# An expert unit on quarters of the array, half-height products for a state-space response, and another order of the last expert block

## The chip, the cores and the metric

The program runs on one core of a Trainium2 chip. The core has a matrix engine (TensorE, PE in the profile, its weight loads apart as PEld), VectorE (DVE), ScalarE (ACT), GpSimd (POOL), and SyncE (SP), which here issues nearly all DMA transfers. The metric is the device time of one execution in microseconds, and its median over runs.

## The reference

Two layers of a diffusion backbone, on 256 latent and 256 context tokens of width 1024, all in float32. Each layer has a mixer of four head groups (two-dimensional neighbourhood attention, grouped attention with rotary positions, a bidirectional diagonal state space, windowed attention with sinks) and a channel mixer. Layer 0 has a dense SwiGLU; layer 1, on the latent tokens alone, has eight experts, of which the router picks two for each token:

```python
logits = jnp.einsum('bld,de->ble', h, w_router, ...) + b_router.astype(F32)
top_val, top_idx = lax.top_k(logits, TOP_K)          # TOP_K = 2
top_w = jax.nn.softmax(top_val, -1)
for e in range(N_EXPERTS):                           # 8 experts, 1024 x 3584
    out = out + gate[..., e:e + 1] * _swiglu(h, w_gate[e], w_up[e], w_down[e])
```

with `_swiglu(h) = (silu(h @ w_gate) * (h @ w_up)) @ w_down`, and behind it a residual sum with a gate vector from the conditioning and a layer norm. The state space needs, for each of 16 channel groups, its response at offsets of up to seven steps in both directions, which the kernel makes from products of the powers of its poles with its input and output matrices.

## The kernel before

**Experts.** The experts are ranked by how many tokens they got. The tokens are gathered into 768 slots, six units of 128. A unit of one expert is whole: units 0, 2 and 3 (largest, second and third expert). Units 1, 4 and 5 are mixed, 64 slots of one expert and 64 of another; unit 1 holds what the largest has beyond 128 (capacity 192) and the smallest (64). What goes past the capacities would be computed by an overflow branch (`overflow`, a test on a register at L1673).

The 3584 hidden columns are cut into seven blocks of 512. In each block the units go in pairs, (1,0), (5,2), (4,3), each a call of `swiglu_units`: gate for both units, up for both, then silu, product, four transposes (L1630), and down. Block 0 goes (5), (4), (1,0), (2,3), the last block (1,0), (5,2), (3), (4). A weight tile is 128 x 2048 (1 MiB); an expert has six in a block. `load` (L1660) issues them on SP in the order of use, into a ring of nine buffers (`ring` in the profile), each freed by its last reader.

A mixed unit works in float32 straight from the ring (L1608): for each of eight k, two matmuls, one per expert, on 64 columns of the array each, 512 wide; each is two instructions in the trace. A whole unit needs its weights split in a high and a low part first, high on ACT (L1571), low on DVE (L1572), and takes three matmuls per k (L1595, L1596, L1598) on all 128 columns. Down has four k in two halves of the 1024 output columns, which DVE adds into `yacc` with the slot's gate (L1744). In block 5, POOL multiplies `yacc` by the layer's gate vector (L1750); in block 6, DVE multiplies each product by it first (L1747). `combine` (L1713) puts a finished unit's `yacc` back on the tokens by matmuls with `DT` (who sits in which slot) and DVE adds the sum to the residual; for the last unit PE loads the tokens into PSUM (L1767) and adds to them there (L1771), and the last layer norm follows.

The order on an engine is laid out by a scheduler when the program is built; `behind(*chain)` keeps the matmuls of successive steps in order.

**State space.** `s5_prep` makes the responses `Ks` for four groups of channels at a time: `CT` is made by six products, copied into an array `X` of fifteen offsets, the upper 64 partitions for one direction and the lower 64 for the other, and eight matmuls (L709) on four quarters of 32 columns give 240 columns, copied by DVE (L715).

**Ahead of layer 0**, the input is scaled and shifted in two halves of four row blocks each: ACT writes the result as the high part `xa` (L1828), DVE scales `xT` itself (L1829), and the low part `xb` is the difference (L1830). L283, L284 and L285 are the first projection's matmuls with these parts.

## Time and profile before

| | |
|---|---|
| median of 3 runs | 1944.35 us (1936.6 to 1945.28) |
| the profiled execution | 1943.62 us, its span 1941.8 us |
| PE busy | 1810.1 us, 93% of the span |
| DVE, ACT, POOL busy | 1071.2, 693.1, 420.8 us |
| DMA traffic | 508.57 MB, mean 262 GB/s |
| granted TensorE clock, mean | 0.967 of full speed |
| matmuls of the mixed units (L1608), gate and up, down | 302.2 and 161.8 us |
| waits of SP for a ring buffer in the expert layer | 448.1 us for L1608, 220.0 us for L1572 |

The expert layer runs from about 1001 to 1929 us. A window tells how busy each engine was in a stretch and what the DMA engines moved; a wait is put down to the engine that released it last; the chain is the succession of work, waits included, that ended last. Times in the rows below count from the span's start.

### The profile page before, as it was taken

Reading aid. Unit: us, or ns where it says so; the run is one execution under the profiler, and the core shown is the slowest. Engines: PE = TensorE matmul, PEld = TensorE weight load, DVE = VectorE, ACT = ScalarE, POOL = GpSimd, SP = SyncE. Lnnn points to the kernel's source line nnn. Section 1 sums busy time; section 2 is a strip of 40 time slices with the busy share of each in tenths; the row PEclk is TensorE's granted clock in tenths of the full one; section 3 lists DMA queues with packets and bytes.
Section 4 is the critical chain, followed back from the end, with each engine's and each line's share of the span. In section 5 each row is a group of like instructions: output and inputs, shape, how many; then the busy total and the mean of one; then the engine's idle time right before and its main releaser. Section 6 shows DMA issues by size and latency. Waiting matters only on the chain.

```text
span 1941.8 us, 23723 instructions
## 1 busy us (share of the span) xinstructions
PE 1810.1 (93%) x8634; PEld 1150.1 (59%) x8634; DVE 1071.2 (55%) x1715; ACT 693.1 (36%) x1077; POOL 420.8 (22%) x368
## 2 busy tenths in 40 slices
PE   6799989799999999899969999999999899999997
PEld 2576547778777777586654475554554454544553
DVE  7978544825456244849673383453543444554473
ACT  2245553422212222436623363342333333423340
POOL 3852232634342422522340000000000000021000
PEclk9899989899999999998979999999999999999999
DMA  8455831224534545251349987999999999999893
GB/s 315 151 164 195 290 133 65 102 95 144 187 133 165 177 172 190 76 188 52 122 164 371 417 333 324 423 420 407 422 400 422 369 379 421 409 398 421 349 378 133
DMA packets 111498, 508.57 MB, mean 262 GB/s; under 512 B 21776, under 2 KB 31632, under 8 KB 68368
## 3 DMA queue, kind: packets, MB, share of 16 engines
q1 hardware_dynamic: 111376, 507.01, 67.1%
q8 instruction: 69, 1.13, 0.2%
q14 instruction: 53, 0.43, 0.1%
HBM read 491.29 MB, written 15.66 MB: 261 GB/s over the span
## 4 chain that ended last, share of the span: by engine, by line
PE 79%; DVE 12%; DMA 3%; issue 2%; POOL 2%; ACT 1%; SPq 1%; DVEq 0%; POOLq 0%; ACTq 0%
PE ps L1608 24%; PE ps L283 8%; PE ps L284 8%; PE ps L285 8%; PE ps L1595 6%; PE ps L1598 6%; PE ps L1596 6%; PE ps L358 2%; PE ps L1096 1%; PE ps L1058 1%; PE ps L1057 1%; PE ps L1630 1%; DMA ring<-in_ada_w_dram 1%; PE ps L1114 1%; PE ps L1713 1%
## 5 line engine op out<-in xcount | busy, mean ns | idle before, releaser
L1572 DVE TENSOR_TENSOR whl<-ring,whl 128x1024 fp32r<-128x1024 f32 x252 | 307.3, 1254 | 114.3 <-ACT whl L1571 105.2
L1571 ACT ACTIVATE whl<-ring 128x1024 fp32r<-128x1024 f32 x252 | 258.0, 1054 | 234.9 <-PE ps L1596 128.8
L1608 PE MATMUL ps<-ring,xg 128*64 128x512 f32 x1344 | 302.2, 599 | 6.0 <-DMA ring<-in_moe_w_dram 6.0
L303 ACT ACTIVATE ring<-ring 128x1024 fp32r<-128x1024 f32 x114 | 120.0, 1059 | 312.7 <-PE ps L284 155.9
L283 PE MATMUL ps<-xa,ring 128*128 128x512 f32 (+1 forms) x576 | 217.2, 378 | 9.0 <-DVE xa L423 8.1
L285 PE MATMUL ps<-xa,ring 128*128 128x512 f32 (+1 forms) x576 | 216.7, 377 | 0.0
L284 PE MATMUL ps<-xb,ring 128*128 128x512 f32 (+1 forms) x576 | 216.2, 376 | 0.3 <-DVE xb L424 0.3
L1608 PEld LDWEIGHTS ps<-ring,xg 128*64 128x64 f32 x1344 | 94.6, 137 | 189.4 <-issue 186.4
L1750 POOL TENSOR_TENSOR yacc<-yacc,gate 128x1024 f32<-128x1024 f32 x6 | 21.1, 3512 | 766.9 <-DVE yacc L1744 734.9
L1608 PE MATMUL ps<-ring,mhT 128*64 128x512 f32 x672 | 161.8, 596 | 1.4 <-ACT mhT L1635 1.4
L305 DVE TENSOR_TENSOR ring<-ring,ring 128x1024 fp32r<-128x1024 f32 x76 | 106.0, 1397 | 90.9 <-ACT ring L303 90.5
L305 POOL TENSOR_TENSOR ring<-ring,ring 128x1024 fp32r<-128x1024 f32 x38 | 95.7, 2518 | 240.5 <-ACT ring L303 212.5
L1595 PE MATMUL ps<-whl,xhl 128*128 128x512 f32 x336 | 135.2, 402 | 0.0
L283 PEld LDWEIGHTS ps<-xa,ring 128*128 128x128 f32 x576 | 110.5, 192 | 36.1 <-DVE xa L423 8.5
L1596 PE MATMUL ps<-whl,xhl 128*128 128x512 f32 x336 | 131.2, 391 | 0.0
L1627 DVE TENSOR_TENSOR mh<-mh,ps 128x512 f32<-128x512 f32 x42 | 28.9, 687 | 185.3 <-PE ps L1608 159.9
L285 PEld LDWEIGHTS ps<-xa,ring 128*128 128x128 f32 x576 | 110.5, 192 | 24.4 <-issue 6.6
L284 PEld LDWEIGHTS ps<-xb,ring 128*128 128x128 f32 x576 | 110.3, 192 | 20.7 <-issue 2.8
L1598 PE MATMUL ps<-whl,xhl 128*128 128x512 f32 x336 | 104.2, 391 | 0.0
L1608 PEld LDWEIGHTS ps<-ring,mhT 128*64 128x64 f32 x672 | 48.4, 137 | 92.9 <-issue 90.6
L1744 DVE SCALAR_TENSOR_TENSOR yacc<-ps,mtab,yacc 128x512 f32<-128x512 f32 x60 | 45.0, 750 | 90.7 <-PE ps L1608 65.8
L1626 ACT ACTIVATE mh<-ps 128x512 f32<-128x512 f32 x42 | 25.0, 595 | 181.2 <-PE ps L1608 122.5
(445 smaller groups left out, 3026.6 us busy)
## 6 DMA issues: line engine op xcount, KB each, us to landing
ring<-in_moe_w_dram SPq DMA_DIRECT2D x334, 1024.0 KB, 10.5
ring<-in_ada_w_dram SPq DMA_DIRECT2D x96, 512.0 KB, 5.7
ring<-in_ffn_gu_dram SPq DMA_DIRECT2D x44, 512.0 KB, 3.5
ring<-in_w_in_dram SPq DMA_DIRECT2D x32, 512.0 KB, 4.7
ring<-in_ffn_d_dram SPq DMA_DIRECT2D x22, 512.0 KB, 3.8
ring<-in_w_out_dram SPq DMA_DIRECT2D x16, 512.0 KB, 3.9
s5CT<-CT SPq DMA_DIRECT2D x8, 512.0 KB, 3.4
s5WB<-WB SPq DMA_DIRECT2D x8, 512.0 KB, 3.0
```

The lines of the kernel that those rows point to most:

```text
L283: PE.matmul(o, a[0], b[0], start=start, stop=False)
L284: PE.matmul(o, a[0], b[1], start=False, stop=False)
L285: PE.matmul(o, a[1], b[0], start=False, stop=stop)
L303: S.activation(hi, r, AF.Copy)
L305: (G if cnt[0] % 3 == 0 else V).tensor_sub(lo, r, hi.bitcast(F32))
L1571: S.activation(t[:, 0], src, AF.Copy)
L1572: V.tensor_sub(t[:, 1], src, t[:, 0].bitcast(F32))
L1595: PE.matmul(o[:, :n], xh[:, k], wh[:, k - k0], start=k == 0, stop=False)
L1596: PE.matmul(o[:, :n], xl[:, k], wh[:, k - k0], start=False, stop=False)
L1598: m = PE.matmul(o[:, :n], xh[:, k], wl[:, k - k0], start=False, stop=k == nks - 1)
L1608: PE.matmul(o[a:b, :n], x[:, k, a:b], w_(w)[:, k - a0], start=k == 0, stop=k == nks - 1, tile_position=pos_)
L1744: V.scalar_tensor_tensor(d, y[hf], g, d, op0=ALU.mult, op1=ALU.add)
```

## The change

Three parts.

**Unit 1 on quarters.** The largest expert's capacity falls to 160 and the smallest's to 32. Unit 1 holds the 32 slots of each twice, in four quarters of 32. A quarter takes half of the 512 columns of a weight tile: quarters 0 and 1 the largest expert's, 2 and 3 the smallest's. `step` issues four matmuls for each k, on 32 columns of the array each, 256 wide; gate and up leave 256 columns for each slot of each quarter, two transposes follow, and `yacc` of unit 1 is 512 wide. `DT` gets a second plane for it, split by the parity of the quarter, and `combine` takes two matmuls of 256 where other units have one of 512.

**State space response.** No `X` and no mask: the products are taken for each direction on its own 64 partitions, 16 matmuls of half height into two PSUM tiles, 128 wide; ACT copies them together and DVE adds the shared offset. In the scaling ahead of layer 0, ACT scales in place and then copies the high part, 512 wide.

**Order.** The last block goes (1,0), (2,3), (5), (4). Combining the units of a finished call is issued between gate and up of the next one (`mid`), the load of the tokens into PSUM ahead of the last unit's transposes (`end`). The gate vector is spread in block 6, behind its first pair (and within the overflow branch), not in block 0; POOL's products in block 5 go, and in block 6 DVE multiplies the whole sum. The overflow branch claims five ring buffers instead of four.

```diff
...
-CAPS = (192, 128, 128, 64, 64, 64, 64, 64)
-BASE = (0, 256, 384, 512, 576, 640, 704, 192)
-NSLOT = sum(CAPS)
-NU = NSLOT // P
-
-UNITS = ((0, 0), (0, 7), (1, 1), (2, 2), (3, 4), (5, 6))
-
-WHOLE = {u for u, rk in enumerate(UNITS) if rk[0] == rk[1]}
+CAPS = (160, 128, 128, 64, 64, 64, 64, 32)
+BASE = (0, 256, 384, 512, 576, 640, 704, 160)
+
+
+UNITS = ((0, 0), (0, 0, 7, 7), (1, 1), (2, 2), (3, 4), (5, 6))
+NU = len(UNITS)
+QUART = {u for u, rk in enumerate(UNITS) if len(rk) == 4}
+
+WHOLE = {u for u, rk in enumerate(UNITS) if len(set(rk)) == 1}
+
+SLOTS = np.arange(NU * P)
+SLOTS[P : 2 * P] = P + np.repeat([0, 0, 32, 32], 32) + np.tile(np.arange(32), 4)
...
-            for i in range(2):
-                V.tensor_copy(X[0:64, i, :, 7:15, :], CT[0:64, i])
-                V.tensor_copy(X[64:128, i, :, 0:8, :], CT[64:128, i])
-            kp = ps("s5")
-            for i in range(2):
-                for g4 in range(4):
-                    PE.matmul(
-                        kp[32 * g4 : 32 * g4 + 32, :240], bb[:, i, 4 * q + g4, :],
-                        X[:, i, g4].rearrange("p m h -> p (m h)"), start=i == 0, stop=i == 1,
-                        tile_position=(0, 32 * g4),
-                    )
+            kp = [ps("s5"), ps("tr")]
+            for r in range(2):
+                dp = slice(64 * r, 64 * r + 64)
+                for i in range(2):
+                    for g4 in range(4):
+                        PE.matmul(
+                            kp[r][32 * g4 : 32 * g4 + 32, :P], bb[dp, i, 4 * q + g4, :],
+                            CT[dp, i, g4].rearrange("p k h -> p (k h)"), start=i == 0, stop=i == 1,
+                            tile_position=(64 * r, 32 * g4),
+                        )
             Ks = T([240], "Ks", nb)
-            V.tensor_copy(Ks, kp[:, :240])
...
+            S.activation(Ks[:, 112:240], kp[0][:, 0:128], AF.Copy)
+            S.activation(Ks[:, 0:112], kp[1][:, 0:112], AF.Copy)
+            V.tensor_add(Ks[:, 112:128], Ks[:, 112:128], kp[1][:, 112:128])
...
+        DT = mp.tile([P, NU + 1, 256], F32R, name="DT")
...
+                if u in QUART:
+                    for i, v in enumerate((u, NU)):
+                        V.tensor_scalar(DT[:, v], tp[:, 0:256], C("par")[:, i : i + 1], None, op0=ALU.mult)
+                else:
...
+                yacc[u] = mp.tile([P, 512 if u in QUART else D], F32, name=nm("yacc"))
...
+                if len(ws) == 2 and ws[0] is ws[1]:
+                    parts = [(0, 128, ws[0], None, slice(0, n))]
+                else:
+                    z = 128 // len(ws)
+                    parts = [
+                        (z * a, z * a + z, w_, (0, z * a), slice(n * (a % 2), n * (a % 2) + n) if z == 32 else slice(0, n))
+                        for a, w_ in enumerate(ws)
+                    ]
...
                 for k in ks:
                     with behind(*chain):
                         ms = [
                             PE.matmul(
-                                o[a:b, :n], x[:, k, a:b], w_(w)[:, k - a0], start=k == 0, stop=k == nks - 1, tile_position=pos_
+                                o[a:b, :n], x(k, a) if callable(x) else x[:, k, a:b], w_(w)[:, k - a0, c],
+                                start=k == 0, stop=k == nks - 1, tile_position=pos_,
                             )
-                            for a, b, w_, pos_ in halves
+                            for a, b, w_, pos_, c in parts
                         ]
...
+                if i == 0 and mid:
+                    mid()
+            if end:
+                end()
+            ys = [
+                [ps("mm" if u else "s5") for _ in range(4 // len(ws))] for u, (_, ws) in enumerate(units)
+            ]
...
+                if len(ws) == 4:
+
+                    hT = lambda k, a, hT=hT: hT[:, k % 2, a // 64 * 64 + k // 2 * 32 :][:, :32]
                 for hf in range(2):
-                    ms = step(ys[u][hf], hT, 4 + hf, ws, 0, range(nk), nk, 512)
+                    if len(ws) == 4:
+                        ms = step(ys[u][0][:, 256 * hf : 256 * hf + 256], hT, 4 + hf, ws, 0, range(nk), nk, 256)
+                    else:
+                        ms = step(ys[u][hf], hT, 4 + hf, ws, 0, range(nk), nk, 512)
...
+                gate = slots[4][:, :D]
+                bcast_rows(gate, adaT[1][:, 40:48, 0])
...
+            units = sorted(units, key=lambda u: u in QUART)
             for h in range(2):
                 for t in range(2):
                     o = ps("mm")
-                    for u in units:
-                        PE.matmul(
-                            o, DT[:, u, 128 * t : 128 * t + 128].bitcast(F32), yacc[u][:, 512 * h : 512 * h + 512],
-                            start=u == units[0], stop=u == units[-1],
-                        )
+                    with behind(*chain):
+                        for u in units:
+                            for c, v, d in ((0, u, 256), (256, NU, 512)) if u in QUART else ((0, u, 512),):
+                                chain[:] = [
+                                    PE.matmul(
+                                        o[:, c:d], DT[:, v, 128 * t : 128 * t + 128].bitcast(F32),
+                                        yacc[u][:, (d - c) * h : (d - c) * (h + 1)],
+                                        start=u == units[0], stop=u == units[-1] and d == 512,
+                                    )
+                                ]
...
+        acc = {}
+
+        def tokens():
+
+            for h in range(2):
+                for t in range(2):
+                    acc[t, h] = ps("tr" if t + h == 2 else "mm")
+                    with behind(*chain):
+                        chain[:] = [
+                            PE.matmul(acc[t, h], ident, res[t + 2][:, 512 * h : 512 * h + 512], start=True, stop=False)
+                        ]
...
-        order = {0: ((5,), (4,), (1, 0), (2, 3)), NB - 1: (PAIRS[0], PAIRS[1], (3,), (4,))}
+        order = {0: ((5,), (4,), (1, 0), (2, 3)), NB - 1: (PAIRS[0], (2, 3), (5,), (4,))}
...
-            ys = swiglu_units([(xg[u], [ws[r] for r in UNITS[u]]) for u in us], 4)
-            if todo:
-                combine(todo)
-                todo = []
+            ys = swiglu_units(
+                [(xg[u], [ws[r] for r in UNITS[u]]) for u in us], 4,
+                partial(combine, todo) if todo else None, tokens if tail else None,
+            )
+            todo = []
+            if (b, us) == (NB - 1, PAIRS[0]):
+                gate = mp.tile([P, D], F32, name="gate")
+                bcast_rows(gate, adaT[1][:, 40:48, 0])
+
+                gateq = mp.tile([P, 512], F32, name="gateq")
+                for a in range(4):
+                    r = slice(32 * a, 32 * a + 32)
+                    G.tensor_copy(
+                        gateq[r].rearrange("p (h x) -> p h x", h=2),
+                        gate[r].rearrange("p (h q x) -> p h q x", h=2, q=2)[:, :, a % 2],
+                    )
             for u, y in zip(us, ys):
                 g = gsl[:, u : u + 1]
-                for hf in range(2):
+                for hf in range(len(y)):
                     c = slice(512 * hf, 512 * hf + 512)
-                    d = yacc[u][:, c]
+                    d, gt = yacc[u][:, c], gateq if u in QUART else gate
                     if b == 0:
                         V.tensor_scalar(d, y[hf], g, None, op0=ALU.mult)
-                    elif b < NB - 1:
+                    else:
                         V.scalar_tensor_tensor(d, y[hf], g, d, op0=ALU.mult, op1=ALU.add)
-                    else:
-                        yg = wtile("mh")
-                        V.tensor_mul(yg, y[hf], gate[:, c])
-                        V.scalar_tensor_tensor(d, yg, g, d, op0=ALU.mult, op1=ALU.add)
-                if b == NB - 2:
-                    G.tensor_mul(yacc[u], yacc[u], gate)
+                    if b == NB - 1:
+                        V.tensor_mul(d, d, gt[:, c])
             if b == NB - 1:
                 todo = list(us)
-            if at == 2:
-                gate = mp.tile([P, D], F32, name="gate")
-                bcast_rows(gate, adaT[1][:, 40:48, 0])
             if (b, us) == (OVER, PAIRS[-1]):
-                overflow([mw() for _ in range(4)])
+                overflow([mw() for _ in range(5)])
...
-                    S.activation(hi[:, f, 256 - 256 * r : 512 - 256 * r], x, AF.Identity, bias=bi, scale=sc)
-                    V.tensor_scalar(x, x, sc, bi, op0=ALU.mult, op1=ALU.add)
+                    S.activation(x, x, AF.Identity, bias=bi, scale=sc)
+                S.activation(hi[:, f], xT[:, f], AF.Copy)
...
```

PE, gate of unit 1 in a middle block, the last of its eight k, and the first rows of unit 0. `ps` is the PSUM tile, `ring` the weight tile's buffer, `xg` the gathered tokens; each row is a matmul of two instructions. Before:

```order
L1608 MATMUL ps_9301<-ring_7757,xg 64x512
L1608 MATMUL ps_9301<-ring_7749,xg 64x512
L1608 MATMUL ps_9301<-ring_7757,xg 64x512
L1608 MATMUL ps_9301<-ring_7749,xg 64x512
L1608 MATMUL ps_9301<-ring_7757,xg 64x512
L1608 MATMUL ps_9301<-ring_7749,xg 64x512
L1595 MATMUL ps_9302<-whl_7758,xhl 128x512
L1596 MATMUL ps_9302<-whl_7758,xhl 128x512
L1595 MATMUL ps_9302<-whl_7758,xhl 128x512
```

After:

```order
L1620 MATMUL ps_9421<-ring_7799,xg 32x256 x2
L1620 MATMUL ps_9421<-ring_7791,xg 32x256 x2
L1620 MATMUL ps_9421<-ring_7799,xg 32x256 x2
L1620 MATMUL ps_9421<-ring_7791,xg 32x256 x2
L1620 MATMUL ps_9421<-ring_7799,xg 32x256 x2
L1620 MATMUL ps_9421<-ring_7791,xg 32x256 x2
L1602 MATMUL ps_9422<-whl_7800,xhl_7808 128x512
L1603 MATMUL ps_9422<-whl_7800,xhl_7808 128x512
L1602 MATMUL ps_9422<-whl_7800,xhl_7808 128x512
```

Where two rows of 64 x 512 stood for a k, one for each expert's tile, there are now two rows of two matmuls of 32 x 256; the rows of unit 0 behind them are the same.

PE, the end of the last unit (unit 4, alone in both): the last rows of up, the combination of the unit before (`yacc`, `DT`), the transposes (of `mh`), the load of the tokens (by the identity, `small`) and the first row of down (`mhT`). Before:

```order
L1608 MATMUL ps_13198<-ring_7750,xg 64x512
L1608 MATMUL ps_13198<-ring_7751,xg 64x512
L1713 MATMUL ps_13251<-yacc_8173,DT 128x512
L1713 MATMUL ps_13254<-yacc_8173,DT 128x512
L1713 MATMUL ps_13257<-yacc_8173,DT 128x512
L1713 MATMUL ps_13260<-yacc_8173,DT 128x512
L1630 MATMUL ps_13223<-small,mh_7673 128x128 x4
L1767 MATMUL ps_13271<-small 128x512
L1767 MATMUL ps_13273<-small 128x512
L1767 MATMUL ps_13275<-small 128x512
L1767 MATMUL ps_13277<-small 128x512
L1608 MATMUL ps_13219<-ring_7752,mhT_7676 64x512
```

After, the end of gate with the combination and the start of up:

```order
L1620 MATMUL ps_13544<-ring_7798,xg 64x512
L1620 MATMUL ps_13544<-ring_7799,xg 64x512
L1745 MATMUL ps_13565<-yacc_7892,DT 128x512
L1745 MATMUL ps_13568<-yacc_7892,DT 128x512
L1745 MATMUL ps_13571<-yacc_7892,DT 128x512
L1745 MATMUL ps_13574<-yacc_7892,DT 128x512
L1620 MATMUL ps_13577<-ring_7791,xg 64x512
L1620 MATMUL ps_13577<-ring_7792,xg 64x512
```

After, the end of up and the start of down:

```order
L1620 MATMUL ps_13577<-ring_7793,xg 64x512
L1620 MATMUL ps_13577<-ring_7794,xg 64x512
L1763 MATMUL ps_13598<-small 128x512
L1763 MATMUL ps_13600<-small 128x512
L1763 MATMUL ps_13602<-small 128x512
L1763 MATMUL ps_13604<-small 128x512
L1650 MATMUL ps_13610<-small,mh_7715 128x128 x4
L1620 MATMUL ps_13606<-ring_7795,mhT_7718 64x512
```

The combination of the unit before has moved from behind up to between gate and up, and the load of the tokens from behind the transposes to ahead of them.

ACT, ahead of layer 0, from the second half of the input's scaling on (`ring` rows are the splits of the first projection's weights, `WB` and `vt` other copies). Before:

```order
L303 ACTIVATE ring_337<-ring_64 128x1024
L303 ACTIVATE ring_338<-ring_65 128x1024
L1828 ACTIVATE xa_267<-xT,small 128x256 x8
L303 ACTIVATE ring_339<-ring_63 128x1024
L737 ACTIVATE WB_708<-ps_709 128x512
L895 ACTIVATE vt_326<-ps_438 128x512
```

After:

```order
L310 ACTIVATE ring_337<-ring_64 128x1024
L310 ACTIVATE ring_338<-ring_65 128x1024
L1873 ACTIVATE xT<-xT,small 128x256 x8
L716 ACTIVATE Ks_691<-ps_673 128x128
L717 ACTIVATE Ks_691<-ps_674 128x112
L1874 ACTIVATE xa_267<-xT 128x512 x4
L740 ACTIVATE WB_704<-ps_705 128x512
L740 ACTIVATE WB_704<-ps_711 128x512
```

The eight scalings of the second half stand at the same place; behind them, two copies of the response `Ks` and four copies of the high part `xa` are new.

## Rows read from the trace of the kernel before

**Rows 1.** Windows: length, busy PE, PEld, DVE, ACT, POOL, clock, DMA share, GB/s.

```profile
1001.00:1102.00 101.00, 91.61 (x467) 47.43 (x468) 45.78 (x121) 31.60 (x60) 4.25 (x3) 0.93 0.96 388
1102.00:1159.00 57.00, 55.30 (x252) 40.78 (x250) 43.74 (x43) 36.99 (x40) 0.00 (x0) 1.00 0.96 369
1159.00:1281.00 122.00, 119.32 (x531) 62.68 (x532) 55.90 (x58) 42.05 (x47) 0.00 (x0) 1.00 0.90 370
1281.00:1404.00 123.00, 120.01 (x530) 62.98 (x526) 56.35 (x58) 42.84 (x48) 0.00 (x0) 1.00 1.00 415
1787.00:1929.00 142.00, 139.20 (x578) 71.84 (x575) 71.21 (x81) 41.07 (x46) 5.54 (x1) 1.00 0.78 314
```

**Rows 2.** Windows of 20 us in the expert layer, the same columns.

```profile
1160.00:1180.00 20.00, 20.00 (x91) 9.48 (x88) 7.87 (x8) 5.33 (x6) 0.00 (x0) 1.00 0.71 283
1280.00:1300.00 20.00, 20.00 (x88) 9.65 (x88) 9.99 (x9) 7.22 (x8) 0.00 (x0) 1.00 1.01 422
1500.00:1520.00 20.00, 19.18 (x88) 9.06 (x85) 8.58 (x9) 8.60 (x10) 0.00 (x0) 1.00 0.82 340
```

**Rows 3.** Waits in the expert layer: engine, line, releaser: total us, times, longest.

```profile
SPq L1660 <- PE ps L1608: 448.1, 140, 10.4
SPq L1660 <- DVE whl L1572: 220.0, 85, 6.5
...
SPq L1673 <- SPq L1673: 12.5, 1, 12.5
...
PE ps L1608 <- DMA ring<-in_moe_w_dram: 6.0, 1, 6.0
```

**Rows 4.** Chain of waits from 1140 us on: start us, us, what.

```profile
1159.22 7.02 PE ps L1608 x32
...
1280.82 7.53 PE ps L1608 x32
...
1522.98 9.64 DMA ring<-in_moe_w_dram
...
1786.78 7.02 PE ps L1608 x32
...
1928.52 2.79 PE ps L1771 x6
```

**Rows 5.** Timeline of PE in block 2: start us, us, instructions.

```profile
1293.95 7.09 PE L1608 MATMUL ps<-ring,xg 128*64 128x512 f32 x32
1300.97 0.50 PE L1595 MATMUL ps<-whl,xhl 128*128 128x512 f32 x1
...
1306.55 0.60 PE L1630 MATMUL ps<-small,mh 128*128 128x128 f32 x4
```

**Rows 6.** Timelines of PE and its weight loads at small matmuls; L709 by line.

```profile
39.92 1.92 PE L358 MATMUL ps<-ring,small 128*32 128x512 f32 x16
...
84.89 1.02 PE L709 MATMUL ps<-tabx,tabs 128*32 128x240 f32 x16
...
84.89 0.56 PEld L709 LDWEIGHTS ps<-tabx,tabs 128*32 128x32 f32 x16 [0.17 <-issue]
...
983.92 3.75 PE L1413 MATMUL ps<-rtab,ntab 128*128 128x8 f32 x32
...
L709 PEld LDWEIGHTS ps<-tabx,tabs x128: 106/109/110, 72.8 to 644.6; 128*32 128x32 f32 x128
```

**Rows 7.** Groups of the page: instructions, busy us and mean ns, idle before.

```profile
L1608 PE MATMUL ps<-ring,xg 128*64 128x512 f32 x1344 | 302.2, 599 | 6.0 <-DMA ring<-in_moe_w_dram 6.0
```

**Rows 8.** Up to 130 us: groups of ACT and DVE by line, and waits.

```profile
L1828 ACT ACTIVATE xa<-xT,small 128x256 fp32r<-128x256 f32 x16 | 8.1, 587 | 13.5 <-DVE small L1822 13.5
...
L1829 DVE TENSOR_SCALAR xT<-xT,small 128x256 f32<-128x256 f32 x16 | 9.6, 628 | 0.0
...
ACT xa L1828 <- DVE small L1822: 13.5, 2, 10.9
...
PE ps L283 <- ACT xa L1828: 11.7, 1, 11.7
```

More of the change, by code (lines that the diff above doesn't have):

```diff
@@ L128, in _pack @@
         put(f"sb{l}", b.transpose(1, 3, 0, 2, 4))
-        put(f"sd{l}", rep(v["ssm_d"][l]))
+        d = np.zeros((4, 32, 4, 16), np.float32)
+        for h in range(16):
+            d[:, h, :, h] = v["ssm_d"][l].reshape(4, 4, 16)[:, :, h].T
+        put(f"sd{l}", d)
         put(f"sc{l}", c.transpose(1, 4, 0, 2, 3))
@@ L1579, in moe, with swiglu_units @@
         chain = []
-        def swiglu_units(units, nk):
+        def swiglu_units(units, nk, mid=None, end=None):
             n = 128 * nk
@@ L1599, in step @@
                     return [m]
-                halves = [(0, 128, ws[0], None)] if ws[0] is ws[1] else [
-                    (64 * a, 64 * a + 64, ws[a], (0, 64 * a)) for a in range(2)
-                ]
-                for a, b, w_, pos_ in halves:
+                if len(ws) == 2 and ws[0] is ws[1]:
[6 more added lines that the diff above has]
+                    ]
+                for _, _, w_, _, _ in parts:
                     w_(w)
@@ L1761, in moe @@
                 SP.dma_start(x, A[n][1:2, :].to_broadcast([P, D]))
-        acc = {}
-        for t in range(2):
-            for h in range(2):
-                acc[t, h] = ps("mm")
-                PE.matmul(acc[t, h], ident, res[t + 2][:, 512 * h : 512 * h + 512], start=True, stop=False)
         for h in range(2):
```

43 lines of the change are left out of this document (18 added, 25 removed).

## The prediction

> **What bounds the kernel now.** The windows by block come first. The expert layer streams 336 weight tiles of 1 MiB, 48 for each of seven blocks, and blocks 1, 2 and 6 take 122, 123 and 142 us, with TensorE (PE) busy for 119, 120 and 139 us of them and the DMA engines' share at 0.90, 1.00 and 0.78 [rows 1]. So PE sets the pace of the last block outright, and the blocks between hover at two limits at once. The 20 us windows give the second limit: where nothing holds the stream it moves 422 GB/s at a share of 1.01 (20 us from 1280) [rows 2]. One tile (1.0486 MB) therefore lands every 2.487 us and a block of 48 tiles costs the stream 119.4 us. It dips to 283 GB/s at 1160 us and to 340 at 1500 us. Over blocks 1 to 5, from 1159.22 to 1786.78 [rows 4], a block took 125.5 us. The waits say who holds it: SP, which issues the loads in order into nine buffers, waits 448.1 us for the mixed units' matmuls and 220.0 us for VectorE's (DVE) split of the whole units, each time for a buffer to come free, while the matmuls of L1608 wait for a landing once, 6.0 us [rows 3]. PE is thus mostly the late one, but by 2 or 3 us a block: 121.6 us from the first matmul of block 1 (1159.22) to that of block 2 (1280.82) against the stream's 119.4 [rows 4]. That nearness decides what the change is worth: a shorter PE block can only be used down to 119.4 us, except in block 0, partly, and in block 6.
>
> **The change part by part.**
>
> *Quarters.* Unit 1 (largest and smallest expert) now issues, for each k, four matmuls of 32 columns and 256 wide instead of two of 64 columns and 512 wide. A phase of eight k of a mixed unit is 32 instructions and 7.02 us, read between its start at 1293.95 and the next unit's at 1300.97 [rows 5], so 0.877 us a k. The same row form with four 32-column tiles is there already: 16 instructions of 512 wide in 1.92 us and 16 of 240 wide in 1.02 us (L358, L709; four column tiles, two passes per matmul) [rows 6]. One instruction 512 wide lasts 0.60 us (L1608 [rows 7]); less that for the last one, 1.92 us leave 1.32 us for three rounds of four, 0.44 us each, so 0.22 for 256 wide. A k has two rounds (two passes): 0.44 us instead of 0.877. Three phases of eight k (gate, up, down) make 24 k a block: 24 × 0.44 = 10.5 us saved, 73.5 us over seven blocks, if all of it lay on the path. The other bound takes a round at a quarter of L709's 1.02 us, the last one's drain and all: 2 × 0.255 × 256/240 = 0.54 us a k and 8.1 us a block. I keep 0.44, since in a phase of 64 instructions the drain is paid once.
>
> Two halves of the cost beside it are small. Silu and product of this unit cover 256 columns instead of 512, transposes go from four to two, yacc's update from two to one; all lie beside matmuls and I take them at nothing (under 1 us a block). The weights streamed are the same 336 tiles. The slots fall to 160 for the largest and 32 for the smallest expert; counting the router's choices on the reference's inputs gives 137 and 20, so the overflow branch stays untaken.
>
> *What the stream leaves of it.* PE's block becomes 121.6 − 10.5 = 111 us, under the stream's 119.4. By bytes, 101 us at 388 GB/s had delivered 37 tiles at 1102 us and 57 us at 369 GB/s brought 57 by 1159 [rows 1]. The quartered unit of block 0 starts at about tile 25 to 36, so I let the stream run freely from 1102 on: block 6's first tiles (number 290) land at 1102 + 253 × 2.487 = 1731. Two losses stay. The overflow test at the end of block 3 holds SP for 12.5 us [rows 3], with 9.64 us of PE waiting for a landing behind it [rows 4]; in the 20 us from 1500 alone the stream lost 20 × (1 − 340/422) = 3.9 us [rows 2]. It now claims five buffers instead of four, so one more of the ring must drain: I take 8 us (4 to 13). And a buffer is freed in bursts, at the ends of phases; with PE as fast as the stream some of them will show: I take 8 us for five blocks, between nothing and what they lost so far, 5 × (125.5 − 121.6) = 19.5 less the test's 4, so 0 to 15. Block 6 then starts on PE at 1731 + 8 + 8 + 1 = 1748 instead of 1786.78.
>
> *Last block.* It is bound by PE before (139.2 of 142 us busy, DMA at 0.78 [rows 1]) and stays so. From 1786.78 to the last matmul phase's end at 1928.52 it takes 141.7 us [rows 4]: three mixed units at 3 × 7.02 = 21.1, three whole ones at 3 × 5.6 = 16.8 (1300.97 to 1306.55 [rows 5]), and 28 us of combines, the token preload, transposes and gaps. The order (1,0), (2,3), (5), (4) only exchanges units, the combines keep their column count (unit 1: two of 256 for one of 512), and the token preload moves ahead of the transposes. Quarters take 10.5 off; the gate's broadcast, moved here from block 0, puts 8 matmuls of 128 on PE and two copies on ACT, 1 us, and the gate product goes from before to after the sum on DVE, 1 us that ends up beside PE in all but the last unit. 141.7 − 10.5 + 2 = 133 us. What follows the last phase (1928.52 to 1941.8, 13.3 us) keeps its work.
>
> *Pool's gate products* of block 5 go. In a block that the stream bounds this gains nothing more than is counted.
>
> *Before the experts.* DVE loses the 16 scalings at L1829 (9.6 us [rows 8]) and the copies into X and Ks; ScalarE (ACT) does the scaling in place and then eight copies of 512, so that its first high part of the second half comes 8 scalings (16 take 8.1 us [rows 8], so 4 us) and two Ks copies later. PE waited 11.7 us for those scalings, and these in turn 10.9 us for DVE [rows 8], which gets there sooner now. A gain of up to 5 us and a loss of up to 5 have equal reasons; I take nothing. The 16 half-height products that replace 8 issue twice the instructions, about half as wide; L709's 1.02 us [rows 6] stand for both, at most 1 us more, four times a layer, beside other work.
>
> **The sum.** 1748 + 133 + 13.3 = 1894.3 us of span; the profiled run's time is 1.8 us over its span (1943.62 and 1941.8), so **1896 us**, 47 below the profiled run, which itself stands 0.7 below the median of 1944.35.
>
> [...] The loads of L709, 16 of 0.11 us, lie within 0.56 us, while the matmuls of the same rows of the array run [rows 6]; taken one after the other behind the matmuls they would need 1.7 us. [...]
>
> **Rivals.**
> (a) *The ring's losses stay as they are* (the dips are refill losses of nine buffers, not PE's lateness). Then only block 0 and block 6 give: block 1 starts 10 us earlier at 1149, the five blocks take their 628 us, and 1149 + 628 + 133 + 13.3 + 1.8 = 1925. For it: the dips to 283 and 340 GB/s [rows 2] and SP's 220 us behind DVE. Against: block 2, 1281 to 1404, ran the stream at 415 GB/s throughout [rows 1].
> (b) *No gain*: the quarter's k stays near 0.877 us, because 64 short instructions in succession (32 matmul passes and 32 loads for each four k) are not supplied at 27 ns each. The slowest row of small matmuls, L1413, has 32 passes and 32 loads of 8 wide in 3.75 us, 59 ns each [rows 6]; at that, a k of 16 instructions is 0.94 us. Time: 1935 to 1955. Against: L709 and L358 keep the pace.
> (c) *Slower*: no weight load hides behind matmuls of the same rows. A k is then 0.44 + 8 × 0.109 [rows 6] = 1.31 us, a block 24 × 0.43 = 10.4 us longer and PE-bound everywhere: 1943.6 + 7 × 10.4 = 2016. It decides from 0.94 us a k on (24 × 7 × 0.06 = 10 us). Against it stands L709, in which they do hide.
> (d) A k between 0.5 and 0.7 us leaves the middle blocks to the stream and costs blocks 0 and 6 up to 6 us each: up to 1908, inside the range.
>
> **Chances.** Forecast with (d), 1876 to 1912: 0.70. (a), 1912 to 1930: 0.17. (b): 0.07. (c): 0.05. Below 1876: 0.01. The low end, 1876, is the sum without bursts (8), with the smaller loss at the test (4) and a prologue gain of 5, which is 1879, and 3 for the last block's gaps; the high end 1926 takes in (a). Half a per cent, 9.7 us, is about what a measurement of this kernel tells from no change: faster 0.88, same 0.06 (most of b), slower 0.06 (c and the rest of b).
>
> **What would show it.** Quarters: the row of L1620, 32 columns, 256 wide, 64 instructions in 3.5 us. Stream: blocks 1 to 5 at 119 to 123 us with 410 GB/s or more, PE at about 0.92 of them, and new rows "PE waits for a landing" of the order of 40 us together. Last block: 133 us at a DMA share like before. The forecast is wrong if the blocks 1 to 5 stay at 125 us with PE no longer busy (a), or if L1620's quarter phase takes 7 us or more (b, c).

## The result

The changed kernel takes 1888.14 us (median of 4 runs, 1885.91 to 1892.88) against 1944.16 us: a ratio of 0.9723, interval 0.9692 to 0.9755. Beside other kernels, in a later series of 5 runs, it took 1890.25 us, a ratio of 0.9734 (0.9713 to 0.9755). Its profiled execution took 1889.4 us with a span of 1887.6. The forecast was 1896, with a range of 1876 to 1926.

**The stream is now the bound.** Two lines of the page, the span in 40 slices: busy share of the DMA engines in tenths, and what they moved. From the 24th slice to the 38th the stream holds 420 to 422 GB/s, but for one slice with the overflow test.

```profile
DMA  7545761224535546252049999999999899999975
GB/s 303 194 138 172 247 227 56 96 90 151 189 106 179 183 156 221 96 186 83 9 139 366 396 421 421 421 420 422 421 420 422 362 422 421 420 421 421 421 304 231
```

The windows of the changed kernel, from the end of block 0 to block 6 (length, busy PE, PEld, DVE, ACT, POOL, clock, DMA share, GB/s); the rows of before are in [rows 1]:

```profile
1100.00:1138.00 38.00, 36.60 (x165) 29.68 (x163) 34.15 (x35) 28.63 (x31) 0.00 (x0) 1.00 1.01 421
1138.00:1251.00 113.00, 109.93 (x624) 61.47 (x622) 55.36 (x56) 41.54 (x47) 0.00 (x0) 1.00 1.01 421
1251.00:1369.00 118.00, 113.25 (x623) 64.05 (x622) 55.16 (x57) 42.41 (x48) 0.00 (x0) 1.00 1.01 421
1369.00:1497.00 128.00, 114.64 (x624) 63.81 (x622) 58.98 (x59) 42.45 (x48) 0.00 (x0) 0.98 0.97 402
1497.00:1614.00 117.00, 111.56 (x612) 61.85 (x613) 51.12 (x52) 41.35 (x47) 0.00 (x0) 0.96 1.01 418
1614.00:1737.00 123.00, 116.92 (x633) 65.97 (x632) 58.14 (x59) 43.56 (x50) 0.00 (x0) 1.00 1.01 421
1737.00:1874.00 137.00, 131.44 (x697) 74.54 (x695) 69.69 (x78) 44.28 (x49) 2.42 (x4) 1.00 0.86 349
```

In blocks 1, 2 and 5 the DMA share is 1.01 throughout, with PE busy for 110, 113 and 117 us. (A PE phase that waits for a tile counts as busy for part of the wait: the first quarter phase of block 2 lasts from 1251.11 to 1256.77 us, 5.66 instead of 3.66, with an idle gap of only 1.39.) Block 3 (128 us) holds the test. Blocks 1 to 5 end at 1737, 599 us after their start; before, they took 628. Block 6 is PE's as before (131.4 of 137 us), its stream at 349 GB/s.

**The quarters.** In PE's timeline a gate or up phase of unit 1 in block 1, and its two halves of down (start us, us, instructions):

```profile
1147.56 3.66 PE L1620 MATMUL ps<-ring,xg 128*32 128x256 f32 x64
...
1157.58 1.94 PE L1620 MATMUL ps<-ring,mhT 128*32 128x256 f32 x32 [0.47 <-ACT mhT L1655]
...
1160.03 1.93 PE L1620 MATMUL ps<-ring,mhT 128*32 128x256 f32 x32
```

64 instructions of 32 columns and 256 wide stand where 32 of 64 columns and 512 wide stood [rows 5]: 3.66 us where there were 7.09. The chain below, which counts the phase up to the next unit's start, has 3.59 us for it, 0.45 us a k.

**Who waits.** SP waits less for the mixed units and more for DVE than in [rows 3], and now also for its own queue's transfers; the rows behind them are the waits for a landing, ACT's before and after, and PE's after (before, 6.0 us [rows 3]):

```profile
SPq L1686 <- PE ps L1620: 346.3, 135, 9.6
SPq L1686 <- DVE whl L1579: 239.8, 114, 8.2
SPq L1686 <- DMA ring<-in_moe_w_dram: 34.5, 58, 1.7
...
SPq L1699 <- SPq L1699: 16.9, 1, 16.9
```

```profile
ACT whl L1571 <- DMA ring<-in_moe_w_dram: 88.6, 24, 10.4
...
ACT whl L1578 <- DMA ring<-in_moe_w_dram: 229.1, 54, 11.4
...
PE ps L1620 <- DMA ring<-in_moe_w_dram: 16.8, 12, 6.9
```

The chain of waits says the same: between the matmuls of before [rows 4] there are now long pieces of DMA.

```profile
1138.37 3.59 PE ps L1620 x64
...
1229.56 15.20 DMA ring<-in_moe_w_dram
...
1343.52 18.31 DMA ring<-in_moe_w_dram
...
1487.24 9.36 DMA ring<-in_moe_w_dram
...
1741.24 1.92 PE ps L1620 x28
...
1874.28 2.79 PE ps L1816 x6
```

The first row is block 1's first quarter phase, 20.9 us earlier than in [rows 4]; the last is the last unit's combination, which follows the last matmul phase and begins 54.2 us earlier. The pieces of 9 to 18 us between them are weight tiles on which the chain hangs.

### The profile page after: what moved, and what is told of

The parts are those of the page before. It is cut to its first block, busy times and chain, and to the rows that moved or that the text cites. A ratio compares the mean times of both kernels' runs of the same rounds, so it can differ in the third digit from the quotient of the medians.

```text
span 1887.6 us, 25174 instructions
## 1 busy us (share of the span) xinstructions
PE 1748.4 (93%) x9428; PEld 1157.4 (61%) x9428; DVE 1022.0 (54%) x1656; ACT 693.0 (37%) x1098; POOL 398.0 (21%) x364
## 4 chain that ended last, share of the span: by engine, by line
PE 64%; DMA 12%; DVE 8%; ACT 1%; issue 1%; SPq 0%; POOL 0%; DVEq 0%; ACTq 0%
PE ps L1620 15%; DMA ring<-in_moe_w_dram 12%; PE ps L290 8%; PE ps L292 8%; PE ps L291 8%; PE ps L1602 5%; PE ps L1605 4%; PE ps L1603 4%; PE ps L365 1%; PE ps L1745 1%; DVE whl L1579 1%; PE ps L1650 1%; PE ps L1061 1%; PE ps L1117 1%; PE ps L1540 1%
## 5 line engine op out<-in xcount | busy, mean ns | idle before, releaser
L1579 DVE TENSOR_TENSOR whl<-ring,whl 128x1024 fp32r<-128x1024 f32 x252 | 298.8, 1220 | 153.8 <-ACT whl L1578 151.5
L1620 PE MATMUL ps<-ring,xg 128*64 128x512 f32 (+1 forms) x1792 | 269.7, 498 | 18.5 <-DMA ring<-in_moe_w_dram 16.8
L1620 PEld LDWEIGHTS ps<-ring,xg 128*64 128x64 f32 (+1 forms) x1792 | 100.6, 125 | 169.4 <-issue 125.1
L1620 PE MATMUL ps<-ring,mhT 128*64 128x512 f32 (+1 forms) x896 | 137.6, 489 | 5.4 <-ACT mhT L1655 5.4
L291 PEld LDWEIGHTS ps<-xb,ring 128*128 128x128 f32 x576 | 111.4, 194 | 20.9 <-issue 3.1
L1802 DVE SCALAR_TENSOR_TENSOR yacc<-ps,mtab,yacc 128x512 f32<-128x512 f32 x66 | 49.5, 749 | 92.6 <-PE ps L1620 66.7
L1647 DVE TENSOR_TENSOR mh<-mh,ps 128x512 f32<-128x512 f32 (+1 forms) x42 | 27.0, 643 | 129.9 <-PE ps L1620 107.1
L1620 PEld LDWEIGHTS ps<-ring,mhT 128*64 128x64 f32 (+1 forms) x896 | 46.0, 123 | 77.4 <-issue 60.0
L365 PE MATMUL ps<-ring,small 128*32 128x512 f32 x384 | 71.9, 647 | 11.0 <-ACT small L342 6.2
```

Of the source, the lines that this page charges most:

```text
L291: PE.matmul(o, a[0], b[1], start=False, stop=False)
L365: PE.matmul(o[32 * j : 32 * j + 32, :], act[:, k, :], w[:, i, :], start=h < 2, stop=h >= 2, tile_position=(0, 32 * j),)
L1579: V.tensor_sub(t[:, 1], src, t[:, 0].bitcast(F32))
L1620: PE.matmul(o[a:b, :n], x(k, a) if callable(x) else x[:, k, a:b], w_(w)[:, k - a0, c], start=k == 0, stop=k == nks - 1, tile_position=pos_,)
```

## The experiments

Ratios are to the kernel before, run on the same chip in the same series.

**Unit 1 on halves again (e1_halves)**, with everything else of the change:

```diff
-CAPS = (160, 128, 128, 64, 64, 64, 64, 32)
+CAPS = (192, 128, 128, 64, 64, 64, 64, 64)
...
-UNITS = ((0, 0), (0, 0, 7, 7), (1, 1), (2, 2), (3, 4), (5, 6))
+UNITS = ((0, 0), (0, 7), (1, 1), (2, 2), (3, 4), (5, 6))
```

> The changed kernel with unit 1 on halves again (capacities 192 and 64, two matmuls of 64 columns and 512 wide a k); the state space part, the new order of the last block and the moved gate stay. Theory (PE's block falls under the stream's only because of the quarters): blocks 1 to 5 go back to 123 to 126 us each, block 0 and block 6 lose 10.5 us each, and what is left of the gain is the 7 us ahead of the experts and some 4 us of POOL's products: 1930 to 1937 us. Rival (the order of the work and the moved combinations carry the gain): 1900 to 1915 us.

1935.54 us, ratio 0.9962 (0.9950 to 0.9974). The windows of its blocks 1, 2 and 5:

```profile
1145.00:1268.00 123.00, 119.63 (x530) 62.09 (x529) 55.30 (x57) 42.35 (x47) 0.00 (x0) 1.00 0.90 370
1268.00:1391.00 123.00, 120.94 (x529) 62.73 (x528) 56.60 (x58) 43.27 (x48) 0.00 (x0) 1.00 0.99 410
...
1649.00:1773.00 124.00, 120.66 (x528) 62.42 (x525) 56.34 (x58) 42.80 (x49) 0.00 (x0) 1.00 0.98 402
```

These are the numbers of before again: PE 120 us of 123 to 124, the stream at 370 to 410 GB/s. (Blocks 3 and 4, with the test between them, took 132 and 126 us, above the 123 to 126 expected of every block.) So the quarters carry all of the gain but 7.5 us, and those are about what the part ahead of the experts is worth (e3_old_prep below).

**The last block in the old order (e2_old_last).**

```diff
-        order = {0: ..., NB - 1: (PAIRS[0], (2, 3), (5,), (4,))}
+        order = {0: ..., NB - 1: (PAIRS[0], PAIRS[1], (3,), (4,))}
```

> The changed kernel with the last block in the old order (1,0), (5,2), (3), (4). Theory (PE-bound block whose units are only exchanged): within 3 us of the changed kernel, 1885 to 1892 us. Rival (two mixed units alone at the end spare PE waits for the splits of whole units): 5 to 10 us longer, 1893 to 1898 us.

1892.16 us, ratio 0.9737 (0.9721 to 0.9753), an interval that overlaps the changed kernel's. Within its profile, block 6 on PE lasts 140.3 us (1733.0 to 1873.3) instead of 136.9. The order is worth some 3 us at most; the number lies at the edge of the theory's range and short of the rival's.

**Preparation and scaling of before (e3_old_prep)**: the state space part and the scaling ahead of layer 0 taken back, the rest kept.

```diff
-                    S.activation(x, x, AF.Identity, bias=bi, scale=sc)
-                S.activation(hi[:, f], xT[:, f], AF.Copy)
+                    S.activation(hi[:, f, 256 - 256 * r : 512 - 256 * r], x, AF.Identity, bias=bi, scale=sc)
+                    V.tensor_scalar(x, x, sc, bi, op0=ALU.mult, op1=ALU.add)
...
+                V.tensor_copy(X[0:64, i, :, 7:15, :], CT[0:64, i])
+                V.tensor_copy(X[64:128, i, :, 0:8, :], CT[64:128, i])
...
+            V.tensor_copy(Ks, kp[:, :240])
```

> The changed kernel with the state space preparation and the scaling ahead of layer 0 as before the change. Theory (these two set the earlier start of the experts): the expert layer's first matmuls come 6 to 8 us later and the whole takes 1893 to 1897 us. Rival (the earlier start comes from another order of the scheduler, not from these parts): 1886 to 1890 us.

1899.11 us, ratio 0.9766 (0.9750 to 0.9782): 9 to 11 us over the two medians of the changed kernel, 6 to 8 by the ratios, and 2 us over the range that the theory gave. Its first weight tile is asked for at 1006.7 us, 12 us later than in the changed kernel, where 6 to 8 were expected. Its transposes of the last mixer's output, the last PE work before the router, end at 985.5 us; before the change they ended at 983.8, in the changed kernel at 977.1, and in eleven other profiles here that have the new preparation at 972.2 to 979.5, 975 in the mean. So this part is worth 4 to 13 us, some 9 in the mean, and profiles of the same code differ by 7 us there. Here 3.5 us more come from behind the transposes: the first tile is asked for 21.2 us after them, in the changed kernel 17.7. How much of that belongs to the old preparation isn't shown: in e1 and e10, whose code there is the changed kernel's, it is 2.3 us more as well. No run separates the scaling from the state space.

**No overflow test (e4_no_test)**, the part for tokens beyond the capacities left out.

```diff
-            if (b, us) == (OVER, PAIRS[-1]):
-                overflow([mw() for _ in range(5)])
```

> The changed kernel without the overflow test and its branch, so without the part for tokens beyond the capacities. Theory (the stream is the bound there, and the test costs it 5 to 7 us): 1881 to 1884 us, and block 3 to 4 at 119 to 120 us. Rival (the nine buffers carry the stream over the test, and PE's own 6 us are hidden by its slack): 1887 to 1890 us.

1885.93 us, ratio 0.9704 (0.9688 to 0.9720). Block 3 and block 4 of it:

```profile
1370.00:1491.00 121.00, 113.73 (x627) 64.21 (x630) 56.22 (x57) 42.46 (x48) 0.00 (x0) 1.00 1.01 421
1491.00:1611.00 120.00, 113.34 (x622) 63.07 (x622) 55.59 (x57) 42.39 (x48) 0.00 (x0) 1.00 1.01 421
```

The stream is whole again: 421 GB/s where the changed kernel had 402 and 418. By the windows the test had cost 128 × (1 − 402/421) = 5.8 us in block 3. The time fell by 2 to 4 us, which lies between the theory's range and the rival's and in neither; the interval doesn't tell 3 from 5. The two profiles, whose first tiles are asked for at the same time (994.7 and 994.8), show where the rest went: without the test block 6 starts on PE 6.6 us earlier (1730.8 instead of 1737.4), and 2 us of it are lost again there, in a first quarter phase that waits for its tiles (8.2 us instead of 5.7).

**Half of each tile (e5_half_tiles)**, from block 1 on.

```diff
-                n = 2 if tail and i == 5 else 4
+                n = 2
...
+                        if k and b and not (tail and i == 5):
+                            continue
```

> The changed kernel that loads, from block 1 on, only half of each weight tile (the other half of the buffer keeps old numbers, so the experts' sums are not those of the reference). All instructions of the engines stay; the stream carries half the bytes. Theory (the stream bounds blocks 1 to 5, PE alone would need 111 to 113 us): blocks 1 to 5 take 111 to 114 us each and the time falls by 35 to 45 us, to 1843 to 1853 us. Rival (PE or the freeing of buffers bounds these blocks): 1880 us or more.

1855.01 us (1853.42 and 1856.59), 2 us over the range given, with the mechanism as expected. Blocks 1, 2, 5 and 6:

```profile
1134.00:1246.00 112.00, 107.73 (x622) 61.17 (x622) 58.14 (x58) 44.96 (x49) 0.00 (x0) 1.00 0.66 228
1246.00:1359.00 113.00, 108.72 (x629) 61.55 (x629) 56.91 (x58) 44.65 (x49) 0.00 (x0) 1.00 0.64 224
...
1592.00:1705.00 113.00, 108.73 (x625) 61.55 (x623) 56.87 (x58) 44.39 (x49) 0.00 (x0) 1.00 0.64 224
1705.00:1838.00 133.00, 128.67 (x695) 74.06 (x694) 67.75 (x76) 43.26 (x48) 3.33 (x4) 1.00 0.50 170
```

PE alone needs 112 to 113 us for a block and 133 us for block 6. The stream moves 170 to 228 GB/s in these windows, and PE waits for a landing only once, for 6.1 us behind the test; so this is what PE would do if it never waited for a tile, and it is the direct measure of the 111 and the 133 in the prediction's sum.

**Less PE work (e6_less_low)**: every second product with the weights' low part left out.

```diff
-                                m = PE.matmul(o[:, :n], xh[:, k], wl[:, k - k0], ...)
+                                if k % 2:
+                                    m = PE.matmul(o[:, :n], xh[:, k], wl[:, k - k0], ...)
```

> The changed kernel without half of the matmuls with the low part of the whole units' weights (every second k, so with less precise sums): some 8.5 us less PE work in each block. Theory (stream-bound from block 1 to 5): these blocks stay at 119 to 121 us, and only blocks 0 and 6 get shorter, by 8 us each at most: 1871 to 1882 us. Rival (PE-bound): seven times 8.5 us less, about 1830 us.

1885.80 us (1882.03 and 1889.58). Blocks 2, 5 and 6:

```profile
1247.00:1366.00 119.00, 109.25 (x590) 55.69 (x588) 55.64 (x57) 42.44 (x48) 0.00 (x0) 1.00 1.01 421
...
1613.00:1733.00 120.00, 108.66 (x589) 56.52 (x587) 55.93 (x58) 42.46 (x48) 0.00 (x0) 0.99 1.01 421
1733.00:1867.00 134.00, 126.07 (x662) 68.12 (x661) 69.30 (x80) 43.83 (x49) 2.42 (x4) 0.99 0.89 360
```

With 4 to 8 us less PE work than in the changed kernel, blocks 2 and 5 stay at 119 and 120 us: they are the stream's. The rival (1830) is out. Block 6 fell by 3.6 us only, not by 8, and the total missed the theory's range from above. PE is busy for 5.4 us less in block 6 (126.1 instead of 131.4), and its first quarter phase takes 8.2 us instead of 5.7, waiting for the stream's tiles.

**Eight buffers (e7_ring8).**

```diff
-        NRAW = 9
+        NRAW = 8
```

> The changed kernel with eight ring buffers instead of nine. Theory (the buffers come free early enough, no loss in bursts): within 4 us of the changed kernel, 1886 to 1892 us, the stream at 419 GB/s or more in blocks 1 to 5. Rival (the ring's depth costs the stream, as the prediction's 8 us for bursts supposed): 8 us or more longer, 1896 to 1910 us, with dips under 400 GB/s.

1895.95 us, ratio 0.9765 (0.9742 to 0.9788): 6 to 8 us over, between the two expectations. The stream kept 421 GB/s in blocks 2 and 5 and 415 in block 1, so there are no dips of the rival's kind there. In its profile the loss lies in two places: from the first tile to block 1 on PE it took 147.1 us (141.5 to 144.5 in six profiles with nine buffers and the same block 0), and blocks 1 to 5 took 601.7 instead of 599.1. With nine buffers nothing is shown that blocks 1, 2 and 5 could gain: the share is 1.01 there already, at 421 GB/s.

**GpSimd's work later (e8_pool_later).** Ahead of the first weight tile stand the router's small VectorE operations. In the changed kernel (and nearly to the hundredth in the kernel before), DVE's timeline there, and POOL's beside it:

```profile
982.61 0.22 DVE L1443 TENSOR_REDUCE mtab<-mtab 128x8 f32<-128x64 f32 x1
982.87 1.96 DVE L1444 TENSOR_SCALAR mtab<-mtab 128x8 f32<-128x8 f32 x1
985.51 0.17 DVE L1454 SCALAR_TENSOR_TENSOR mtab<-ps,rtab 128x8 f32<-128x8 f32 x1 [0.69 <-PE ps L1448]
...
987.46 2.01 DVE L1457 TENSOR_TENSOR mtab<-mtab,rtab 128x64 f32<-128x64 f32 x1
989.50 2.27 DVE L1459 TENSOR_TENSOR mtab<-mtab,rtab 128x64 f32<-128x64 f32 x1
991.80 0.22 DVE L1460 TENSOR_REDUCE mtab<-mtab 128x8 f32<-128x64 f32 x1
992.06 1.95 DVE L1461 CAST eidi<-mtab 128x8 int32<-128x8 f32 x1
```

```profile
982.42 4.66 POOL L1277 TENSOR_TENSOR xk<-xh,xk 128x1024 fp32r<-128x1024 f32 x2 [7.00 <-ACT xk L1276]
987.05 4.63 POOL L1281 TENSOR_TENSOR small<-xh,lng 128x1024 f32<-128x1024 f32 x2
991.65 4.64 POOL L1282 TENSOR_TENSOR small<-small,lnb 128x1024 f32<-128x1024 f32 x2
```

A reduction over 128 x 64 takes 0.22 us; products, sums and copies no larger take 1.5 to 2.3 us, each about as long as one of the two GpSimd operations in a row of POOL's (2.3 us). The run moves POOL's product, sum and scaling of the residual behind the first expert unit:

```diff
-            with behind(last["lo"]):
+            def post(y):
+                col = tab(1)
+                V.tensor_scalar(col, y, 0.0, ALPHA, op0=ALU.mult, op1=ALU.add)
+                for g in gb:
+                    G.tensor_scalar(g, g, col, None, op0=ALU.mult)
...
-                    prescale(i + 2)
...
+            if at == 0:
+                cur["post"](yacc[5][:, 0:1])
```

> The changed kernel with GpSimd's work on the residual (product with the layer norm's gain, sum with its offset, scaling) moved from beside the router's small VectorE operations to after the first expert unit. Theory (VectorE's operations of 128 x 64 take 2 us instead of 0.22 while GpSimd works on 128 x 1024, and the router's chain sets the start of the weight stream): the first weight tile is asked for 5 to 9 us earlier after the router's start, and the time is 1879 to 1884 us. Rival (the slow operations are not due to GpSimd, or the stream's earlier start is lost in block 0): 1886 to 1890 us.

1882.31 us, ratio 0.9691 (0.9668 to 0.9715), within the theory's range, though the interval touches the changed kernel's (0.9692 to 0.9755). The first tile is asked for 14.6 us after the transposes instead of 17.7, so 3.1 us earlier and not 5 to 9, and the first gathering matmul comes 18.6 us after them instead of 25.5. What is left of POOL ahead of the router (the low part of the tokens) still holds two operations for 2.3 us each.

**The changed kernel again (e9_after_again).**

> The changed kernel once more, beside the three others of this call: 1885 to 1893 us, ratio to the kernel before 0.970 to 0.975. Its expert layer starts where it may: the first weight tile at 996 to 1000 us after the span's start, by the five profiles that share the code ahead of it.

1890.25 us, as given above. The time came as expected; the first tile is asked for at 989.9 us, ahead of the 996 to 1000 that were expected, and 17.7 us after the transposes as in the other profile, where it is at 994.7.

**The gate vector early (e10_gate_early)**: spread behind block 1's first pair.

```diff
-            if (b, us) == (NB - 1, PAIRS[0]):
+            if (b, us) == (1, PAIRS[0]):
...
-                overflow([mw() for _ in range(5)])
+                overflow([mw() for _ in range(4)])
```

> The changed kernel with the gate vector spread behind block 1's first pair (where PE waits for the stream anyway) instead of in block 6, the quarters' gate product taken from it in four pieces, and four ring buffers for the overflow branch instead of five. Theory (PE's 2.2 us leave the last block, which is PE-bound; the test costs the stream 1 us less): block 6 at 134 to 135 us, 1884 to 1887 us, 2 to 4 us under the changed kernel beside it. Rival (the broadcast was hidden in the wait for the first tiles of block 6): no difference, under 1 us.

1886.17 us, ratio 0.9722 (0.9703 to 0.9741), 4 us under the run beside it, with intervals that overlap. Its block 6:

```profile
1733.00:1868.00 135.00, 129.19 (x679) 72.67 (x679) 71.54 (x82) 43.11 (x47) 0.00 (x0) 1.00 0.88 355
```

PE is busy for 129.2 us there, 2.2 less, and the block lasts 134.8 instead of 136.8 us (1732.1 to 1868.9 in the run beside it). That is clearer than the total: from the start of block 6 to the end of the span both profiles of the changed kernel take 150.2 us, this one 148.1 and that of e11 147.9. Blocks 1 to 5, which hold the broadcast now, take 598.0 us here and 599.2 in the run beside it, so it costs nothing there. The test loses as much with four buffers: the three tiles that land next behind it (193 to 195) take 12.1 us here and 12.2 in the run beside it, against 7.5 without the test (e4). So the term is the broadcast's alone.

**Both, and the low part on VectorE (e11_both).**

```diff
-                last["lo"] = G.tensor_sub(xk[:, i, 1], xhs[i], xk[:, i, 0].bitcast(F32))
...
+            def low():
+                for i in range(2):
+                    V.tensor_sub(xk[:, i, 1], xhs[i], xk[:, i, 0].bitcast(F32))
...
         late = behind(last["ei"])
+        cur["low"]()
```

> The early gate vector together with GpSimd's residual work behind the first expert unit, and the low part of the gathered tokens taken by VectorE right after the experts' order is known instead of by GpSimd ahead of it. Theory: no operation of 128 x 64 in the router over 0.3 us, the first weight tile 3 us earlier than in the run with only the residual work moved (against the router's first matmul), 1874 to 1880 us. Rival (the chain's start is then set by something else, or block 0 on PE takes the gain back): 1881 to 1885 us.

1875.59 us, ratio 0.9663 (0.9645 to 0.9682), faster than both kernels. The router's operations of the rows above, now:

```profile
984.67 0.22 DVE L1454 TENSOR_REDUCE mtab<-mtab 128x8 f32<-128x64 f32 x1
984.93 0.17 DVE L1455 TENSOR_SCALAR mtab<-mtab 128x8 f32<-128x8 f32 x1
...
986.73 0.23 DVE L1468 TENSOR_TENSOR mtab<-mtab,rtab 128x64 f32<-128x64 f32 x1
986.99 0.27 DVE L1470 TENSOR_TENSOR mtab<-mtab,rtab 128x64 f32<-128x64 f32 x1
987.29 0.22 DVE L1471 TENSOR_REDUCE mtab<-mtab 128x8 f32<-128x64 f32 x1
987.55 0.17 DVE L1472 CAST eidi<-mtab 128x8 int32<-128x8 f32 x1
```

All of them take 0.17 to 0.27 us, and the first tile is asked for 10.9 us after the transposes. SP's first loads, in the changed kernel and here (the transposes ended at 977.1 and 977.7):

```profile
994.74 5.38 SPq L1686 DMA_DIRECT2D ring<-in_moe_w_dram  x9
```

```profile
988.52 5.94 SPq L1698 DMA_DIRECT2D ring<-in_moe_w_dram  x9
```

**The whole units first in the last block (e12_both_whole_first).**

```diff
-        order = {0: ..., NB - 1: (PAIRS[0], (2, 3), (5,), (4,))}
+        order = {0: ..., NB - 1: ((2, 3), PAIRS[0], (5,), (4,))}
```

> The same with the last block in the order (2,3), (1,0), (5), (4), so that the stream's tiles meet 34 us of whole units first and the quartered unit comes when the stream is ahead. Theory (block 6 loses 2 to 3 us waiting for tiles in the quartered unit): 1 to 3 us under the run before it. Rival (what comes first waits for its splits as long): the same or up to 3 us more.

1879.67 us, ratio 0.9685 (0.9664 to 0.9706): 4 us over the run before it, with intervals that overlap. There is no gain; it is the rival's side, a little beyond its range. Tile 290 landed 2.2 us later in its profile, and the end is 2.7 us later, so the order itself is worth nothing that these two profiles show.

## Why the prediction was right, step by step

| step | predicted | measured |
|---|---|---|
| a k of the quartered unit | 0.44 us | 0.45 us |
| PE's block without waits | 111 us | 112 to 113 us (e5) |
| stream in blocks 1 to 5 | 119.4 us a block at 422 GB/s | 421 GB/s, 119.6 to 120.9 us for 48 tiles outside the test |
| losses outside the test | 8 us | 3.8 us: tiles 38 to 290 in 633.0 us without the test (e4), for 629.2 |
| the overflow test | 8 us (4 to 13) | 5.8 us |
| ahead of the experts | 0 (up to 5 either way) | −6.9 us: first tile at 994.7, before at 1001.7 |
| block 0, first tile to block 1 on PE | −10.5 | 157.5 to 143.6: −13.9 us |
| block 6 starts on PE | 1748 | 1737.4 |
| block 6 | 133 us | 136.9 us |
| from there to the end | 13.3 us | 13.3 us |
| span | 1894.3 | 1887.6 |

**What bounds the kernel.** The turn from PE to the stream in blocks 1 to 5 is shown from three sides: halves bring PE's bound back (e1), half the bytes bring the blocks to 112 (e5), and less PE work leaves them where they are (e6). Of the 52.5 us of PE time saved in blocks 1 to 5, 28.5 arrived. That the sum gives 1748 − 1149 = 599 us for them, and they took 599, is partly luck. The stream was 14.1 us ahead when PE began block 1 (tile 48 landed at 1124.2, block 1 began at 1138.3), 6.3 us at block 2 and 6.2 at block 6. So block 1 still ran at PE's own pace (113 us), and the 240 tiles of the five blocks took the stream 607 us, 10 more than 5 × 119.4. The prediction had losses of 16 us and a lead of some 20 at block 1 (tile 48 at 1102 + 11 × 2.487 = 1129, block 1 at 1149); the two errors cancel.

**The signs that it named.** The quarter phase came as said (3.66 us for 3.5), and so did the rate. The blocks took 113 to 128 us and not 119 to 123, PE was busy for 0.90 to 0.97 of them and not for 0.92, and its idle time before landings is 16.8 us, not 40: much of its waiting lies within phases that count as busy. In the reading of before, the 9.64 us that the prediction calls PE's wait behind the test are a tile's piece of the chain [rows 4]; PE's own wait was 6.0 us [rows 3]. The sum doesn't use it.

**Quarters.** The row form with four column tiles, read from two short bursts [rows 6], holds for 64 instructions in succession. Rivals (b), (c) and (d) are out: 0.45 us a k. The loads do hide: 64 of 0.11 us (this phase's own mean) would make 7.0 us one after the other; they lie within 3.18 us, and the whole phase, matmuls included, takes 3.66.

**Rival (a)**, that the ring's losses stay, is out: 421 GB/s in every window that the test doesn't reach into. The dips of before were PE's lateness, as the stream's wait rows had said, and the 8 us for bursts were 4 too many. The reason given for a dearer test, a fifth buffer to drain, isn't borne out: with four the test costs as much (e10).

**Ahead of the experts** is the term that was mis-sized: nothing was taken, with ±5; it is −6.9 in this pair of profiles, and about 9 in the means of e3's comparison. The argument weighed DVE's relief against ACT's later copies and found equal reasons. In the windows from 0 to 130 us, DVE's busy time had fallen from 106 to 84 us with PE's 98 grown to 104; so the relief was probably the larger one, though no run separates the two.

**Block 0** gained 13.9 us and not 10.5. The gate vector's broadcast had stood in block 0; the prediction charged it to block 6, as 1 us where PE needs 2.2, and forgot to take it out of block 0. **Block 6** without waits is 133.3 us long (e5), the forecast's number, but the stream brings its first tiles late: the first gate phase of the quarters takes 5.7 us there instead of 3.7, with a wait of 1.5 us for a landing inside it. The sum let block 6 run at PE's pace from its first tile on.

So the sum was right to 7 us with the bound, the saving and the last block in place, helped by errors of opposite sign. Its own terms run along the stream. Tile 37 landed at 1096.8 us and not by 1102 (−5); the 253 tiles behind it took 639.4 us, 10.2 over the free rate, and not 16 over (−6); block 6 took 136.9 us and not 133 (+4). The −5 has an error of its own in it: in the kernel before, tile 37 landed at 1106.2, 4 us later than the sum's division of bytes by tiles had it, since that counts tiles still under way; against this the stream is 9.4 us earlier, 6.9 of them from ahead of the experts.

## What to carry to other kernels

Where two limits are 2% apart, the gain from easing one is cut at the other: work out both for each stage, and count the full saving only in the stages (here the first and the last) where the other limit has slack. Work that has to be done somewhere then belongs into the stages that wait: 2.2 us of broadcast cost 2 us in the last block and nothing in block 1. And in a kernel whose long phase is a stream, look at what sets the stream's first transfer. Here it was a chain of tiny VectorE operations beside GpSimd's: with them freed the first tile is asked for 6.8 us sooner behind the transposes (10.9 instead of 17.7), where the order of the last block was worth 3 us at most.

## What the runs showed of the hardware

VectorE's operations of 128 x 64 and less took 1.5 to 2.3 us instead of 0.17 to 0.27 while GpSimd worked through operations of 128 x 1024 in SBUF, one GpSimd operation (2.3 us) for each; reductions stayed at 0.22 us among them, and the one with an input in PSUM (L1454) at 0.17. The same line (L1444) took 0.16 us at 981.76 us, ahead of the first of these GpSimd operations (982.42), and 1.96 us at 982.87. With GpSimd's work away, all of them were short (0.17 to 0.27 us in e11). What makes them long isn't shown beyond this.

Four matmuls on quarters of the array's columns, each with its own weights, ran for 64 instructions in succession: 3.66 us for a phase in which one instruction lasts 0.38 us by the profile (24.3 us one after the other), half of the time of two on halves (7.09 us [rows 5]). The stream held 421 GB/s for blocks on end (1, 2 and 5, and 3 and 4 in e4) at a DMA share of 1.01; no slice of the page of either kernel is over 423 GB/s.
